# Another order of visits in a weight-gradient kernel that walks PSUM banks by hand

## The chip, the cores and the metric

The kernel runs on one core of a Trainium2 chip. The metric is the device time of one execution in microseconds; the median of three executions of the kernel before is 164.53 us (164.5 to 164.6). The span of the profiled execution, from its first to its last instruction, is 163.0 us.

## The reference

```python
batch, m, k, n = 16, 512, 1024, 768
input:       (batch, m, k) float32
grad_output: (batch, m, n) float32

grad_weight = np.einsum('bmk,bmn->kn', input, grad_output)   # (1024, 768) float32
```

All 16 x 512 = 8192 rows are contracted, so the work is one product of a 1024 x 8192 matrix with an 8192 x 768 matrix.

## The kernel before, in words

**Rows.** The 8192 rows are loaded as 32 loads of 256 rows (u = 0 to 31), input as tile `xp` and gradient as tile `gp`, cast to bf16 on the way by transfers that GpSimd issues (L107 and L108; the first rows come by L82 to L85 and L112 to L114, and rows 0 to 255 of the input are rounded on the chip, L205 to L216 and L361 to L367). `LOADS` says what a load becomes: `s`, two single items of 128 rows each, or `P`, one pair item of 256 rows. Loads 0 to 7 give the single items 0 to 15, loads 8 to 29 the pair items 16 to 37, loads 30 and 31 the single items 38 to 41. Up to 14 loads are held at a time.

**Products.** The output is split into four blocks: A and B are the upper 512 rows, C and D the lower; A and C the left 384 columns, B and D the right. A single item needs a product for each of the four blocks. A pair item is contracted with seven products in place of eight, in the manner of a fast 2 x 2 matrix scheme: `A`, `D`, `m`, `n`, `o`, `p`, `q` (L219 to L240). For that VectorE first makes six sums of a pair item's parts (`sum_g1` to `sum_x3`, L126 to L155, here called a sextet): g1, g2, g3 need the gradient, x1, x2, x3 the input. `o` and `p` need g3; `n` and `q` need x1; `m` needs x1, x2, g1, g2; `A` and `D` need x3 and g1. The five products `m` to `q` are collected in `macc`, and at the end 24 shares (L173 to L190) add them to the blocks in `acc`. Their order is the list `SHARES`.

**Visits.** Each product has 512 x 384 results, which are four PSUM banks (q = 0 to 3) of 128 x 384. Eight banks make two slots of four. A product occupies a slot while its visits run: a visit multiplies some further items of its product, bank by bank, and a closing visit evacuates the banks to `acc` or `macc`. When a product is opened again later, its old sum is either copied into the bank by ScalarE first (L267; the evacuation is then a ScalarE copy, L300), or TensorE starts from zero and VectorE adds the bank to the old sum (L304). Each tile matmul is 128 x 128 by 128 x 384 (L286); there are 936, whatever the order. In the very last visit the last bank is split in two (L333 to L347).

**What sets the order.** Everything is issued in the order of the list `ORDER`, one visit after another, and each engine works through its own queue in that order. A step such as `2A16:3!1,0,3,0` reads: first 2 of VectorE's sums or shares (`fill`, L199); then visit product A up to its item number 16 (in its own list of items: all 42 for A and D, the 20 single ones for B and C, the 22 pairs for `m` to `q`); where this opens the product, 3 of the four banks are done by ScalarE; `!` closes it, with 1, 0, 3 and 0 further sums or shares put ahead of the evacuations of banks 0 to 3. `+n` opens C on top of the finished sum `n`. An item of a visit can only be multiplied when its load has landed and its sums are made; an opened bank must have been evacuated by the visit that held it before. The part that joins VectorE's two kinds of work is

```python
def shut(q):
    fill(ahead[q])
    bank, _, act = banks[q]
    dst = sum_of(p, q)
    if act:
        nc.scalar.copy(out=dst, in_=bank)
    elif fresh[p]:
        nc.vector.tensor_copy(out=dst, in_=bank)
    else:
        nc.vector.tensor_add(out=dst, in0=bank, in1=dst)
```

The list was found by a search over an account of when each transfer lands and how long each operation takes; the kernel holds only its result.

Of the kernel before, what the change touches and what calls it, by code (L numbers as in the profile page):

```python
# [13 lines left out]


ORDER = (
    "C1:4!0,0,0,0 D1:1 A2:2!0,0,0,0 D2!0,0,0,0 B2:2 C3:1 B4!0,0,0,0 C4!0,0,0,0 A3 A4!0,0,0,0 D4 "
    "D5 A6:4!0,0,0,0 D6!0,0,0,0 B6:1!0,0,0,0 C7!0,0,0,0 A8:1 D8:1 D10!0,0,0,0 A10!0,0,0,0 B10:2 "
    "B12!0,0,0,0 C12 D13:3!0,0,0,0 A13:1!0,0,0,0 C16!0,0,0,1 1B16:4!0,0,0,0 D14 2A16:3!1,0,3,0 "
    "D17 3m2:4!2,0,0,1 D18!0,0,0,0 n2:4!1,0,1,0 1q2:4!0,3,0,0 2o3:2 p2:3 o4!0,0,0,1 p4 1A19:4 "  # L20
    "3A20!0,0,3,0 p5 q5!0,0,0,0 m5:4!1,0,2,0 p6!1,1,0,1 n6!0,0,0,1 o6:4 D22:4 9D23 4o8!1,0,0,0 "
    "A24:2!0,0,0,0 2q8:1 q9!1,0,0,0 D25!0,2,0,0 p7 1p8 p10!1,0,2,0 m7:4 m10!0,0,6,0 o11!0,1,0,0 "
    "3n10:4 p12:3!3,1,0,0 n12!1,0,2,0 q12:1 m13:4!6,0,0,0 q13!0,0,0,0 1A28 1A29!0,1,0,2 D30:4 "
    "o14:4 o15!0,1,1,0 D31!0,2,4,0 2p16 1A32:3!0,0,0,0 3n17!0,2,0,1 p17!0,0,0,0 2D33:3 q16:4 "
    "1q18!0,0,1,1 2m16 2D35!0,0,7,0 m19 2m20!0,0,0,0 o20:4 5p19:2 1p21 o21 o22!0,2,0,0 "
    "1p22!0,0,0,3 A36 m22:4!0,0,0,1 A38 q20:3 q22!3,0,0,0 1A40 n20:4 1n22!0,0,0,3 3A42!0,0,1,0 "
    "C20:0+n!0,0,0,1 B20:4!3,1,1,1 D42!0,0,1,0 "
).split()


SHARES = (
    "l20 l21 l22 l23 t10 t11 t12 t13 t20 t21 t22 t30 t31 t32 t23 t33 l30 l10 l11 l12 l31 l32 l13 "
    "l33 "
).split()

# [366 lines left out]
```

## Time and profile before

| | |
|---|---|
| time, median of 3 | 164.53 us |
| span of the profiled execution | 163.0 us |
| TensorE clock granted | 0.999 |
| mean of one tile matmul, start to end (they overlap) | 326 ns |
| addition of a bank to its sum on VectorE (L304) | 549 ns, 96 of them in the largest groups |
| copy of a bank by ScalarE (L300), into a bank (L267) | 490 to 501 ns, 501 to 510 ns |
| sums of a sextet: g1, g2, g3, x1, x2, x3 | 548, 348, 548, 681, 415, 681 ns |
| moved by the DMA engines | 33.40 MB, mean 205 GB/s |

A duration in the profile runs from an instruction's start to its end, and the next one on the same engine may start before that end, so the distances between starts are shorter than the durations. "Idle before" is time in which an engine had nothing to run, with what ended it. For loads the trace also has the time at which the completion of each arrived; "landing" means that time. All times count from the start of the span.

### The profile page before, as it was taken

To read this page: it belongs to the slowest core of one execution; us is meant where nothing else is said; L and a number is where in the kernel's file an instruction comes from. 1 tells how busy PE (TensorE), PEld (TensorE's weight loads), DVE (VectorE), ACT (ScalarE), POOL (GpSimd) and SP (SyncE) were. 2 spreads that over 40 slices of the span, in tenths; PEclk is the share of its full clock that TensorE was granted. 3 is DMA by queue.
4 is the path that set the end of the run, shared out by engine and by line. 5 is a ranking of instruction groups with operands and counts; after the bars stand their busy time and mean duration, and the time that the engine had idled before them with its cause. 6 is when DMAs were issued, how large, how long until landed. Compare 5 with 4: busy or idle time off the path is not lost.

```text
span 163.0 us, 2759 instructions
## 1 busy us (share of the span) xinstructions
PE 158.0 (97%) x955; PEld 93.2 (57%) x955; DVE 130.7 (80%) x271; ACT 96.3 (59%) x226; POOL 34.6 (21%) x69
## 2 busy tenths in 40 slices
PE   8999998999999999999999999999999999999992
PEld 2366664666655656555656555665656566665661
DVE  0458585405969987999799998995998999999992
ACT  3844831347676467955477598549365427877720
POOL 7442222212222222122222222122222000000000
PEclk9999999999999999999999999999999999999999
DMA  5999999999999999999999999999999999600894
GB/s 174 293 212 212 213 212 215 217 211 211 214 215 210 212 211 216 214 211 212 213 214 214 213 211 216 214 211 210 213 216 212 211 213 215 135 4 0 308 322 146
DMA packets 12398, 33.40 MB, mean 205 GB/s; under 512 B 1376, under 2 KB 4192, under 8 KB 12384
## 3 DMA queue, kind: packets, MB, share of 16 engines
q0 software_dynamic: 9360, 28.64, 88.8%
q1 hardware_dynamic: 2592, 3.47, 6.0%
q10 hardware_dynamic: 432, 1.11, 1.8%
q8 instruction: 7, 0.11, 0.3%
q14 instruction: 7, 0.06, 0.1%
HBM read 58.72 MB, written 3.15 MB: 380 GB/s over the span
## 4 chain that ended last, share of the span: by engine, by line
PE 82%; DMA 14%; POOL 1%; issue 1%; DVE 0%; POOLq 0%
PE bank L286 81%; DMA xp<-in_input_dram 14%; POOL gp L112 1%; PE bank L337 0%; DVE acc L345 0%; POOLq L386 0%
## 5 line engine op out<-in xcount | busy, mean ns | idle before, releaser
L286 PEld LDWEIGHTS <-xp 128*128 128x128 bf16 x665 | 64.8, 98 | 45.3 <-DMA xp<-in_input_dram 1.1
L286 PE MATMUL bank<-gp,xp 128*128 128x384 bf16 x492 | 84.0, 326 | 1.1 <-DMA xp<-in_input_dram 0.7
L304 DVE TENSOR_TENSOR acc<-bank,acc 128x384 f32<-128x384 f32 x58 | 29.2, 549 | 16.5 <-PE bank L286 15.9
L300 ACT COPY macc<-bank 128x384 f32<-128x384 f32 x67 | 27.6, 501 | 22.4 <-PE bank L286 22.2
L300 ACT COPY acc<-bank 128x384 f32<-128x384 f32 x54 | 24.0, 490 | 21.2 <-PE bank L286 20.9
L286 PEld LDWEIGHTS <-xe 128*128 128x128 bf16 x264 | 25.7, 98 | 17.5 <-DVE xe L150 0.5
L286 PE MATMUL bank<-ge,xp 128*128 128x384 bf16 x173 | 31.3, 326 | 0.0
L286 PE MATMUL bank<-gp,xe 128*128 128x384 bf16 x176 | 30.5, 326 | 0.0
L108 POOL DMA_DIRECT2D xp<-in_input_dram x30 | 15.9, 530 | 52.3 <-DMA xp<-in_input_dram 28.5
L267 ACT COPY bank<-macc 128x384 f32<-128x384 f32 x50 | 22.6, 510 | 6.2 <-DVE macc L304 4.2
L267 ACT COPY bank<-acc 128x384 f32<-128x384 f32 x45 | 20.4, 501 | 6.7 <-DVE acc L304 3.4
L107 POOL DMA_DIRECT2D gp<-in_grad_output_dram x30 | 15.9, 531 | 38.2 <-DMA gp<-in_grad_output_dram 17.2
L304 DVE TENSOR_TENSOR macc<-bank,macc 128x384 f32<-128x384 f32 x38 | 19.1, 549 | 2.9 <-PE bank L286 1.8
L190 DVE TENSOR_TENSOR acc<-acc,macc 128x768 f32<-128x768 f32 (+1 forms) x24 | 16.5, 748 | 0.0
L286 PE MATMUL bank<-ge,xe 128*128 128x384 bf16 x88 | 15.6, 326 | 0.0
L146 DVE TENSOR_TENSOR xe<-xp 128x1024 bf16<-128x1024 bf16 x22 | 15.0, 681 | 0.7 <-DMA xp<-in_input_dram 0.7
L155 DVE TENSOR_TENSOR xp<-xp 128x1024 bf16<-128x1024 bf16 x22 | 15.0, 681 | 0.0
L132 DVE TENSOR_TENSOR ge<-gp 128x768 bf16<-128x768 bf16 x22 | 12.1, 548 | 0.1
L141 DVE TENSOR_TENSOR gp<-gp 128x768 bf16<-128x768 bf16 x22 | 12.1, 548 | 0.0
L150 DVE TENSOR_TENSOR xe<-xp 128x512 bf16<-128x512 bf16 x22 | 9.1, 415 | 0.0
L136 DVE TENSOR_TENSOR ge<-gp 128x384 bf16<-128x384 bf16 x22 | 7.7, 348 | 0.0
L302 DVE COPY acc<-bank 128x384 f32<-128x384 f32 x7 | 3.5, 550 | 2.5 <-PE bank L286 2.4
(19 smaller groups left out, 21.3 us busy)
## 6 DMA issues: line engine op xcount, KB each, us to landing
xp<-in_input_dram POOLq DMA_DIRECT2D x30, 512.0 KB, 16.8
gp<-in_grad_output_dram POOLq DMA_DIRECT2D x30, 384.0 KB, 16.7
out_dram<-acc SPq DMA_DIRECT2D x15, 192.0 KB, 2.4
xf<-in_input_dram ACTq DMA_DIRECT2D x2, 512.0 KB, 4.9
gp<-in_grad_output_dram POOLq DMA_DIRECT2D x3, 192.0 KB, 6.5
xp<-in_input_dram POOLq DMA_DIRECT2D x2, 256.0 KB, 7.8
gf<-in_grad_output_dram SPq DMA_DIRECT2D x2, 192.0 KB, 4.3
out_dram<-acc SPq DMA_DIRECT2D x1, 128.0 KB, 1.8
```

What stands on the lines that cost most here:

```text
L107: nc.gpsimd.dma_start(out=gp, in_=G[rows, :].rearrange("(p m) n -> p m n", m=2))
L108: nc.gpsimd.dma_start(out=xp, in_=X[rows, :].rearrange("(p m) k -> p m k", m=2))
L132: nc.vector.tensor_add(out=ge[:, 0:2, :], in0=g[:, :, 0, :], in1=g[:, :, 1, :])
L141: nc.vector.tensor_sub(out=g[:, 1:3, :], in0=g[:, 1:3, :], in1=g[:, 3::-3, :])
L146: nc.vector.tensor_add(out=xe[:, 0:2, :].rearrange("p a k -> p (a k)"), in0=xp[:, 0, :], in1=xp[:, 1, :])
L150: nc.vector.tensor_add(out=extra[i][0][:, 2, :], in0=xp[:, 0, 0:KH], in1=xp[:, 1, KH:K])
L155: nc.vector.tensor_sub(out=x[:, 1:3, :], in0=x[:, 1:3, :], in1=x[:, 0::3, :])
L190: op(out=dst, in0=dst, in1=src)
L267: nc.scalar.copy(out=bank, in_=sum_of(p, q))
L286: nc.tensor.matmul(bank, stat, mov, start=opening and j == 0 and not carried, stop=close and j == len(items_now) - 1, skip_group_check=car ...
L300: nc.scalar.copy(out=dst, in_=bank)
L304: nc.vector.tensor_add(out=dst, in0=bank, in1=dst)
```

## The change

`ORDER` and `SHARES` are replaced by other lists; no other line is touched. The new lists come from the same search over an account that differs in two points: it has one transfer landing late, and the third quarter opening later (the words of the change; the diff doesn't say which quarter is meant). The aim is an order that doesn't ask for data before they are there.

Both orders end with the same three products (C, B, D), load the same data in the same sequence and run the same number of tile matmuls. The first difference is in the second visit (`A1` in place of `D1`); around the loads 3 to 5 the single products come in another order; in the middle the products of the pairs are visited in another sequence, with the sums and the shares put at other places among them.

```diff
 ORDER = (
-    "C1:4!0,0,0,0 D1:1 A2:2!0,0,0,0 D2!0,0,0,0 B2:2 C3:1 B4!0,0,0,0 C4!0,0,0,0 A3 A4!0,0,0,0 D4 "
-    "D5 A6:4!0,0,0,0 D6!0,0,0,0 B6:1!0,0,0,0 C7!0,0,0,0 A8:1 D8:1 D10!0,0,0,0 A10!0,0,0,0 B10:2 "
-    "B12!0,0,0,0 C12 D13:3!0,0,0,0 A13:1!0,0,0,0 C16!0,0,0,1 1B16:4!0,0,0,0 D14 2A16:3!1,0,3,0 "
-    "D17 3m2:4!2,0,0,1 D18!0,0,0,0 n2:4!1,0,1,0 1q2:4!0,3,0,0 2o3:2 p2:3 o4!0,0,0,1 p4 1A19:4 "
-    "3A20!0,0,3,0 p5 q5!0,0,0,0 m5:4!1,0,2,0 p6!1,1,0,1 n6!0,0,0,1 o6:4 D22:4 9D23 4o8!1,0,0,0 "
-    "A24:2!0,0,0,0 2q8:1 q9!1,0,0,0 D25!0,2,0,0 p7 1p8 p10!1,0,2,0 m7:4 m10!0,0,6,0 o11!0,1,0,0 "
-    "3n10:4 p12:3!3,1,0,0 n12!1,0,2,0 q12:1 m13:4!6,0,0,0 q13!0,0,0,0 1A28 1A29!0,1,0,2 D30:4 "
-    "o14:4 o15!0,1,1,0 D31!0,2,4,0 2p16 1A32:3!0,0,0,0 3n17!0,2,0,1 p17!0,0,0,0 2D33:3 q16:4 "
-    "1q18!0,0,1,1 2m16 2D35!0,0,7,0 m19 2m20!0,0,0,0 o20:4 5p19:2 1p21 o21 o22!0,2,0,0 "
-    "1p22!0,0,0,3 A36 m22:4!0,0,0,1 A38 q20:3 q22!3,0,0,0 1A40 n20:4 1n22!0,0,0,3 3A42!0,0,1,0 "
-    "C20:0+n!0,0,0,1 B20:4!3,1,1,1 D42!0,0,1,0 "
+    "C1:4!0,0,0,0 A1 D2:3!0,0,0,0 A2!0,0,0,0 B2:1 C3:3 C4!0,0,0,0 B4!0,0,0,0 A3 A4!0,0,0,0 D4 "
+    "B6:3!0,0,0,0 D6 C6:1 C8!0,0,0,0 A8!0,0,0,0 D8 B7:2!0,0,0,0 D10!0,0,0,0 B10:2!0,0,0,0 "
+    "A10!0,0,0,0 B12:2!0,0,0,0 C10 A12 A14!0,0,0,0 D14:2!0,0,0,0 C16!0,2,1,1 B16:4!1,0,1,1 D16 "
+    "A17:4!2,1,1,1 q2:3!0,1,1,1 m2:3!0,0,0,0 D17 p3:3!2,0,1,1 D18!0,0,0,0 n3:4!0,0,0,2 o3:4 "
+    "3A20:3!3,0,0,1 o4 q5:3!2,0,1,2 m5!0,0,0,0 o6!1,1,0,1 n6!1,0,0,0 p6:4 D20:3 D21 5D23 "
+    "3p8!1,1,1,0 A24:2!1,0,1,1 m8:1 2m9!1,0,0,0 D25!0,0,0,1 o9 2o10!2,0,0,0 q9:4 q10!3,1,0,0 "
+    "p11!1,0,0,0 n11:4 5o12:4!3,0,1,0 m12:1 n12!5,0,0,0 m13!0,0,0,0 A27 q13:4!4,0,2,0 A30!1,0,0,1 "
+    "D29:3 p12:4 1p15 D30 6p16!2,1,0,0 D31!0,0,0,1 o16!2,0,1,0 n17:3!0,1,2,2 m16 A32:3!4,0,0,1 "
+    "m18!0,0,0,0 q18 4D35:4!3,0,2,1 q20!0,0,0,0 p19:3 o17:4 3p21 o21 6o22!2,1,0,0 p22!0,0,0,0 A36 "
+    "q22:4!3,1,0,1 1A39 m22:4!1,1,1,1 A40 n22:3!1,2,0,1 A42!2,0,0,0 C20:0+n!0,0,0,1 B20:4!0,1,2,2 "
+    "D42!2,0,0,0 "
 ).split()
...
 SHARES = (
-    "l20 l21 l22 l23 t10 t11 t12 t13 t20 t21 t22 t30 t31 t32 t23 t33 l30 l10 l11 l12 l31 l32 l13 "
+    "l20 l21 l22 l23 t20 t21 t22 t23 t10 t11 t12 t13 t30 t31 t32 t33 l10 l11 l12 l13 l30 l31 l32 "
     "l33 "
 ).split()
```

## The prediction

> **What bounds the kernel now.** I read the engine totals first, then the chain that ended last, the waits, TensorE's timeline around the one long wait, and the busy time by stretches.
>
> ```profile
> PE 158.0 (97%) x955; PEld 93.2 (57%) x955; DVE 130.7 (80%) x271; ACT 96.3 (59%) x226; POOL 34.6 (21%) x69
> ...
> q8 instruction: 7, 0.11, 0.3%
> ```
>
> From the chain (start, duration, what):
>
> ```profile
> 2.41 7.21 DMA xp<-in_input_dram
> 9.62 0.28 issue
> 9.90 15.93 DMA xp<-in_input_dram
> 25.84 0.05 issue
> 25.88 132.81 PE bank L286 x813
> 158.69 0.78 PE bank L337 x7
> ```
>
> The waits (who, for whom: us in total, times, longest; the other engines wait for TensorE, and TensorE's weight loads for one transfer) and TensorE's timeline:
>
> ```profile
> DVE acc L304 <- PE bank L286: 15.9, 10, 3.7
> ...
> PEld L286 <- DMA xp<-in_input_dram: 1.1, 1, 1.1
> ```
>
> ```profile
> 16.69 8.45 PE L286 MATMUL bank<-gp,xp 128*128 128x384 bf16 x51
> 25.88 4.40 PE L286 MATMUL bank<-gp,xp 128*128 128x384 bf16 x26 [0.74 <-DMA xp<-in_input_dram]
> ```
>
> Until 25.88 us the end is set by a load (pair u=4: items 8 and 9); after it TensorE runs 813 matmuls without a long stop. The records start 162 or 163 ns apart when nothing waits. I use 0.1624 us and call p the number of tile matmuls ahead of one. The first (p=0) starts at 5.44 us, so 5.44 + 0.1624p is the time without any wait, and the **lag** is what a matmul starts later than that. From the records: lag 0.70 at p=88, 1.60 at p=116 (25.88 us), 1.84 at p=364, 1.94 at p=540, 2.14 at p=740, 2.22 at p=908. So before loses 0.70 at the start, 0.90 to the late load, and 0.62 afterwards: 0.53 in nine waits of 0.02 to 0.13 us, the rest because 0.1624 is a little short. These 2.22 us are all that an order of visits can win: there are 936 tile matmuls, 152.0 us, in any order.
>
> VectorE is the next engine to look at (busy time by stretches; columns PE, PEld, DVE, ACT, POOL):
>
> ```profile
> 100.00:110.00 10.00, 10.00 (x63) 6.03 (x62) 9.86 (x22) 5.54 (x14) 2.37 (x5) 1.00 1.07 213
> ...
> 140.00:150.00 10.00, 10.00 (x63) 6.01 (x62) 9.79 (x15) 7.24 (x19) 0.00 (x0) 1.00 0.13 27
> ```
>
> It is nearly full there, though TensorE hardly waits for it.
>
> **What the Trainium skill says.** "TensorE: Matmul & The Clock Gate", Back-to-back issue gap, prices one matmul of N columns at N/2.4 + 2.5 ns: 162.5 ns for 384, and the trace has 162 to 163. "Perfetto Trace Analysis", Identifying the Most-Contended Engine, warns that matmul busy time doesn't tell how near the limit TensorE is; hence start distances here, not the 97%. "DMA: Bandwidth & Descriptors", Why a DMA increments its semaphore by 16, says that 16 engines finish a transfer independently and only all 16 make it landed; its Queues, rings and completion order says that an engine takes turns between queues, packet by packet. The trace fits both: a 16 KB packet of the instruction queue starts at 21.27 us and takes 945 ns, and the gradient load of u=4 lands at 23.48, 2.98 us after the one before it where 1.85 is usual. The loads behind it keep their 4.31 us a pair but stay that much late. Which DMA engine it was the records don't say, so the cause is a reading. The diff doesn't touch what I take for the trigger (the length of TensorE's program), so I keep the landings of before: u=3 at 20.49, u=4 at 25.84, then 4.31 us a pair; u=29 (item 37) at 133.70, u=31 at 142.33.
>
> **The change part by part.** Nothing is removed but waits: 936 matmuls, the 22 sextets of sums and the 24 shares stay. Counted from the two strings: openings 57 to 58; preloads by ScalarE 99 both; evacuations by ScalarE 121 to 120; by VectorE 107 to 112 (97 to 101 additions, 10 to 11 copies). VectorE starts such evacuations 0.465 us apart, so it gets 5 x 0.465 = 2.3 us more work. Walking each engine's queue with TensorE's positions as the clock:
>
> *Start.* A1 instead of D1 takes the left half of the gradient, which is rounded earlier, so the 0.30 us wait for the right half (6.57 us) goes. But D2 then meets item 1's gradient, landed at 7.46: its second matmul (p=9) starts at 7.51 where before had 7.58. Gain 0.07.
>
> *The late transfer.* C8 (p=88) comes at 7.51 + 79 x 0.1624 = 20.34, 20.37 with a 0.03 wait of C3 for a bank, and needs u=3: 20.54 with 0.05 from landing to matmul. Lag 0.81: a wait of 0.17 that before doesn't have (C7 reaches that load two matmuls later). Behind it on TensorE stand A8, D8 and B7, and the evacuations of C8 on VectorE wait with them; none of these has work that something else is short of then. D10, the first to need u=4, moves from p=116 to p=124, behind A8, D8 and B7, which use u=3 and older: 20.54 + 36 x 0.1624 = 26.39 us, after the landing. The 0.74 us of idle time is gone. At p=124 the lag is 0.81 against 1.62.
>
> *The middle.* With lag 0.81 loads are met with less in hand. VectorE's sextet starts as the load lands, and I compare its ends with the first matmul that needs them (starts 0.469, 0.269, 0.469, 0.602, 0.336, 0.602 apart). A24: x of item 23 lands at 73.30, its three sums end 73.35 + 0.60 + 0.34 + 0.68 = 74.97, 75.01 with the semaphore; p=423 comes at 74.95: 0.06 to 0.10 late. p11: the four additions of o10 and four sums put item 26 (p=498) 0.09 late. m13 0.12, A30 0.17, n17 0.16 are late against a lag of 0.81, but these too wait for landings, and vanish once the lag has grown by 0.2. Everything else has room. The same walk of the order of before gives 0.05, 0.10, 0.06, 0.07, 0.05 and 0.06 where its trace has small waits, so I add 0.10 for what it misses: lag at the end 0.81 + 0.10 + 0.09 + 0.05 (matmuls are nearer 162.45) + 0.10 = 1.15.
>
> *Item 37.* o22 (p=784, both orders) can't run before 133.75, which is a lag of 0.99 whatever comes earlier. So the lag at the end lies between 1.0 and 2.22, unless the new order has large waits of its own.
>
> *The end.* From the landing of x37 VectorE has 3 sums (1.54), 12 wide shares (0.869), 12 narrow ones (0.469) and 15 evacuations: 1.54 + 10.43 + 5.63 + 6.98 = 24.6 us, to 158.3. TensorE ends near 158.6, so the last addition still waits for it, and the tail (additions, stores, 3.4 us after the last matmul's start) is the same. The buffers of pairs and sums are freed over 15 us before they are needed in both orders, so no load starts later.
>
> Sum: 164.53 - (2.22 - 1.15) = 163.46, say **163.5 us**.
>
> **The rivals.** *The waits come back (chance 0.12).* Visits that open a slot with none in between go from 6 to 8, with A17, q2, m2 three in a row, and the sextets are laid out with 0.1 us to spare. For it: the nine small waits of before. If they double to 1.2 us, the lag ends at 0.81 + 1.2 = 2.0: 164.3, still less than before but near no change. *The late transfer moves or comes twice (0.09).* If instruction fetches hit one DMA engine again, landings are 1 us later, o22 is held to lag 2.0 and the time is 164.3 to 164.5. Against it: no such shift in the six later 16 KB packets. *VectorE becomes the bound (0.06), slower.* Its 2.3 us of new work all lengthen the path: 163.5 + 2.3 = 165.8. For it: 9.8 of 10 us busy in two stretches. Against it: its sums wait for landings in my walk, 1.2 us ahead of x37 alone. *All small waits hide (0.03):* lag 1.0, 163.3.
>
> **How the numbers follow.** My forecast has 0.70. Range 163.1 to 164.3: from 0.2 under the o22 bound (landings moved by that much) to the half-lost gain. Below 164.2 counts as faster: 0.70, 0.03 and most of the first rival, 0.84; the same 0.10; slower 0.06.
>
> **What would show it.** No TensorE wait for a load near 25 us; one of about 0.2 near 20.5; a lag of 0.8 at p=124; u=4 still at 25.8; item 37 met by TensorE with no time in hand at 133.8; VectorE busy near 133. Wrong would be a second late transfer, a wait over 0.2 us for VectorE between 40 and 130 us, or VectorE running past TensorE at the end.

## The result

The changed kernel takes 164.06 us (median of 6 executions, 163.87 to 164.22), the kernel before 164.55: a ratio of 0.9968, 95% interval 0.9955 to 0.9981. In a second comparison, on another occasion, it was 163.95 against 164.67, 0.9955 (0.9941 to 0.9968). So it is faster by 0.5 to 0.7 us, where 1.05 had been forecast. The direction and most of the mechanism were right, and the time lies in the range; the gain is about half to two thirds of the forecast. One execution in the experiments below (of the kernel with the old opening and the new rest) took 429.87 us; no figure here includes it, and its cause is not known.

### The profile page after: what moved, and what is told of

Read it like the earlier page. It is cut to its first block, busy times and chain, and to the rows that moved or that the text cites. A ratio compares the mean times of both kernels' runs of the same rounds, so it can differ in the third digit from the quotient of the medians.

```text
span 162.3 us, 2773 instructions
## 1 busy us (share of the span) xinstructions
PE 158.0 (97%) x955; PEld 93.6 (58%) x955; DVE 134.1 (83%) x276; ACT 96.4 (59%) x225; POOL 34.7 (21%) x69
## 4 chain that ended last, share of the span: by engine, by line
PE 92%; DMA 4%; DVE 1%; issue 1%; ACT 0%; ACTq 0%; POOLq 0%
PE bank L286 92%; DMA gp<-in_grad_output_dram 4%; PE bank L337 0%; DVE acc L345 0%; DVE acc L304 0%; ACT bank L267 0%; ACTq L267 0%; POOLq L386 0%
## 5 line engine op out<-in xcount | busy, mean ns | idle before, releaser
L286 PE MATMUL bank<-gp,xp 128*128 128x384 bf16 x492 | 85.2, 327 | 0.4 <-ACT bank L267 0.2
L300 ACT COPY macc<-bank 128x384 f32<-128x384 f32 x67 | 29.1, 494 | 27.6 <-PE bank L286 27.2
L304 DVE TENSOR_TENSOR acc<-bank,acc 128x384 f32<-128x384 f32 x62 | 31.5, 550 | 12.7 <-PE bank L286 12.2
L286 PEld LDWEIGHTS <-xe 128*128 128x128 bf16 x264 | 25.8, 98 | 17.1
L300 ACT COPY acc<-bank 128x384 f32<-128x384 f32 x53 | 23.5, 486 | 19.0 <-PE bank L286 18.7
L286 PE MATMUL bank<-ge,xp 128*128 128x384 bf16 x173 | 32.1, 326 | 0.0
L267 ACT COPY bank<-macc 128x384 f32<-128x384 f32 x50 | 21.9, 515 | 0.1
L90 PE MATMUL bank<-const-bfloat16-1.0 128*128 128x512 bf16 (+1 forms) x12 | 4.6, 577 | 0.8 <-PEq L386 0.8
```

What stands on the lines that cost most here:

```text
L267: nc.scalar.copy(out=bank, in_=sum_of(p, q))
L286: nc.tensor.matmul(bank, stat, mov, start=opening and j == 0 and not carried, stop=close and j == len(items_now) - 1, skip_group_check=car ...
```

## The profile after

Engine totals and the instruction queue, from the page of the changed kernel:

```profile
PE 158.0 (97%) x955; PEld 93.6 (58%) x955; DVE 134.1 (83%) x276; ACT 96.4 (59%) x225; POOL 34.7 (21%) x69
...
q8 instruction: 7, 0.11, 0.3%
```

TensorE has the same instructions and the same busy time. VectorE has 5 instructions and 3.4 us more (134.1 for 130.7), ScalarE one copy less. The counts are those of the prediction; its 2.3 us for VectorE were reckoned from the distances between starts. The chain that ended last (start, duration, what):

```profile
1.23 6.45 DMA gp<-in_grad_output_dram
7.67 0.04 issue
7.72 13.03 PE bank L286 x79
20.75 0.01 issue
20.75 15.79 PE bank L286 x96
36.54 0.55 DVE acc L304
37.09 0.02 issue
37.11 0.02 ACTq L267
37.12 0.35 issue
37.47 0.49 ACT bank L267
37.97 0.04 issue
38.01 120.05 PE bank L286 x737
```

Before, loads stood in the chain until 25.88 us. Now it leaves them at 7.67 us, where item 1's gradient lands; after that TensorE gives way only twice in this chain, at 20.75 us (the load 3 that C8 meets) and at 38.01 us. The second is new: VectorE adds a bank of A14, ScalarE copies D14's old sum into the freed bank, and 0.35 us of that is "issue", time for which the profile shows no reason. TensorE's timeline shows no wait where it had stood idle for 0.74 us, near 25 us:

```profile
16.68 13.51 PE L286 MATMUL bank<-gp,xp 128*128 128x384 bf16 x81
```

and two of its waits (who, for whom: us in total, times, longest):

```profile
PEld L286 <- DMA xp<-in_input_dram: 0.6, 2, 0.4
PE bank L286 <- ACT bank L267: 0.2, 1, 0.2
```

The second is the wait at 38.01 us (p=192, in D14). The view counts from the end of the matmul ahead, which overlaps the next one. From start to start the distance is 0.346 us longer than the usual 0.1624, and this is what the text below calls a wait.

VectorE in the two stretches that were shown of before (columns PE, PEld, DVE, ACT, POOL):

```profile
100.00:110.00 10.00, 10.00 (x64) 6.01 (x62) 8.96 (x20) 5.34 (x13) 2.61 (x5) 1.00 1.07 213
140.00:150.00 10.00, 10.00 (x64) 6.04 (x62) 10.00 (x16) 8.14 (x20) 0.00 (x0) 1.00 0.14 28
```

In the second of them VectorE is busy all the time, and TensorE never waits for it there.

Lags, as the prediction defined them (start of the matmul less 5.44 + 0.1624p), from the records:

| | before | forecast | changed, first trace | changed, second trace |
|---|---|---|---|---|
| p=9 (item 1's gradient has landed) | 0.68 | 0.61 | 0.82 | 0.61 |
| p=88 (C7 or C8) | 0.70 | 0.81 | 1.02 | 0.81 |
| p=124 (behind the late load) | 1.62 | 0.81 | 1.03 | 0.83 |
| p=200 (behind D14) | 1.62 | 0.81 | 1.39 | 1.18 |
| p=784 (item 37) | 2.16 | 0.99 or more | 1.57 | 1.37 |
| p=908 (last visit) | 2.22 | 1.15 | 1.58 | 1.38 |

The executions in these traces took 164.76 us (before), 164.11 and 163.95. In all ten traces of this study the time of the execution is 162.53 to 162.67 us plus its lag at p=908, so the lag accounts for nearly all of the differences. Before's trace is not a typical one: its execution is 0.2 us above the median.

The second trace follows the forecast to 0.02 us until p=124, then loses 0.35 between there and p=200, where nothing had been expected, and 0.20 in the remaining 708 matmuls, where before lost 0.60. The first trace has the same and 0.21 more from its start, because item 1's gradient landed at 7.67 us and not at 7.47.

## The experiments

**The changed kernel again.** No edit. Is the wait at D14 the program's?

> The changed kernel once more, nothing altered. Theory 1 (the wait at D14 belongs to the program: ScalarE refills banks 2 and 3 of D14 only when VectorE has added A14's last banks): TensorE again waits about 0.35 us near 38.0 us, and the time is 164.0 to 164.2. Rival (an accident of that one execution): the wait there is under 0.05 us and the profiled time nearer 163.7. In both: the second wait at the start is ended by the landing of item 1's gradient, which came at 7.67 us in the changed kernel's trace and at 7.46 in that of before; if the difference is chance it will fall anywhere between.

Measured 163.95 us, 0.9955 (0.9941 to 0.9968), the second comparison above. The wait at p=192 is 0.346 us in both traces. ScalarE's timeline in this one (idle time and what ended it in brackets):

```profile
37.27 0.89 ACT L267 COPY bank<-acc 128x384 f32<-128x384 f32 x2 [4.22 <-DVE acc L304]
```

The refill starts 0.37 us after the record of its wait (36.90 us), again. So the wait is the program's. The landing of item 1's gradient is not: 7.47 us here, and between 7.38 and 7.96 in the ten traces of this study, which issue it at the same time.

**D14 without ScalarE.**

```diff
- ... A14!0,0,0,0 D14:2!0,0,0,0 C16!0,2,1,1 ...
+ ... A14!0,0,0,0 D14!0,0,0,0 C16!0,2,1,1 ...
```

> The changed kernel with D14 opened without ScalarE: its four banks start from zero and VectorE adds them, 2 more additions (0.93 us) and 4 fewer copies on ScalarE. Theory 1 (the refill's chain costs 0.35 us and nothing takes it back): the wait at 38.0 us is gone and the time falls by 0.3 to 163.7 or 163.8. Rival (what TensorE wins there it loses again to loads and sums before item 37, or VectorE's two additions delay the sums that C16 carries): 164.0 to 164.2, with new waits between 40 and 134 us.

Measured 163.57 us, 0.9939 (0.9927 to 0.9952), less than the changed kernel in the same comparison by 0.38 us (medians) or 0.26 (ratios). TensorE runs through. The longest piece of its chain is

```profile
8.00 150.01 PE bank L286 x920
```

where the changed kernel's chain had pieces of 79, 96 and 737 matmuls. Between p=200 and 908 it loses 0.20 us, as the changed kernel does. The profiled execution itself took 164.09; in it item 1's gradient landed at 7.96 us, 0.5 later than in the changed kernel's second trace, which is about the whole difference. TensorE therefore reaches p=200 no earlier than in that trace (lag 1.33 against 1.18); that an earlier arrival is kept as well, the next run shows. This run takes the refill away altogether, so it doesn't tell whether the chain or the 0.35 us of "issue" was at fault.

**Why ScalarE is late.** In the changed kernel's two traces, and in those of two orders below that keep D14's refill, the late instruction is number 63 of ScalarE's records, counted from 0 with its waits and DMA issues. Number 319 in the changed kernel (near 154.3 us) and number 191 in three of the orders below start as late after the record of their wait: steps of 128. The edit puts two instructions ahead:

```diff
+    spare = accp.tile([P, 8], f32, name="spare")
...
+        if n == 10:
+            for c in range(2):
+                nc.scalar.copy(out=spare[:, c : c + 1], in_=nc.const_aps.tensor(1.0, (P, 1), bf16))
```

> The changed kernel with two copies of one column into a tile that nothing reads, on ScalarE ahead of D4 (near 14.6 us, where ScalarE is idle). In three traces the refill of D14's bank 2 starts 0.37 us after the semaphore it waits for, where other refills take 0.03 to 0.09, and it is ScalarE's instruction 63 counted from 0 each time; instruction 319 = 63 + 256, and in one order 191 = 63 + 128, show the same. Theory (ScalarE changes to its next 128 instructions there, whatever they do): with two more instructions ahead the delay goes to the copy before (near 32.5 us, which nobody waits for), the wait at D14 falls from 0.35 to under 0.06, and the time by 0.3, to 163.65. Rival (the delay belongs to this refill, say to 4 us of idle time before it or to its bank): wait and time as in the changed kernel, 163.95.

Measured 163.62 us, 0.9943 (0.9930 to 0.9955). ScalarE's timeline, in the changed kernel's first trace and in this one (where all lines of the file are one or more further down):

```profile
32.39 0.86 ACT L300 COPY acc<-bank 128x384 f32<-128x384 f32 x2 [1.00 <-PE bank L286]
37.47 0.90 ACT L267 COPY bank<-acc 128x384 f32<-128x384 f32 x2 [4.22 <-DVE acc L304]
```

```profile
32.20 0.48 ACT L301 COPY acc<-bank 128x384 f32<-128x384 f32 x1 [1.00 <-PE bank L287]
32.84 0.48 ACT L301 COPY acc<-bank 128x384 f32<-128x384 f32 x1 [0.17 <-ACT acc L301]
36.97 0.94 ACT L268 COPY bank<-acc 128x384 f32<-128x384 f32 x2 [3.64 <-DVE acc L305]
```

The copy before, which ran on without a gap in the changed kernel, now starts 0.17 us after the end of the one ahead, and it is number 63. The refill now starts 0.06 us after the record of its wait (36.91 us), although ScalarE was again idle for over 3 us before it, so neither the idle time nor the bank is the reason. TensorE's wait at p=192 falls from 0.346 to 0.036, and its chain is again one piece of 920 matmuls. Its lag is 0.88 at p=200 and 1.07 at p=908: again 0.20 lost, so the lead is kept. More work on ScalarE made the kernel 0.2 (by the ratios) to 0.3 us (by the medians) faster.

The ten traces together say when the delay shows. Nine times a copy with one of these numbers stands directly behind a record that waits for a semaphore, on an idle ScalarE; all nine start 0.32 to 0.37 us after the end of that record. With other numbers there are 358 such copies, and all start within 0.05 us. (Twice more, in orders below, number 191 stands behind such a record while the copy ahead still runs.) Where the number falls into a run of copies without gaps (63 in the kernel before), no delay is seen, nor where the copy itself waits without a record ahead (191 in this run starts 0.02 us after its semaphore).

**The old opening with the new rest.**

```diff
- the new order up to D14
+ the old order up to B12 C12 D13:3!0,0,0,0 A13:1!0,0,0,0
  C16!0,2,1,1 B16:4!1,0,1,1 D16 A17:4!2,1,1,1 q2:3!0,1,1,1 ...
```

> The kernel before up to D13 and A13, and from C16 on the new order (D16 and A17 take one more item each to bridge). If the lags add up: the middle of the new order has 0.20 us of waits where the old has 0.60, so 0.4 less than before, 164.15; TensorE still waits 0.74 us for load 4 near 25.1 us. Rival (the middle is only free of waits because the new opening gives it other sums in hand): 164.5, no change.

Measured 164.18 us, 0.9968 (0.9958 to 0.9979). The stop for load 4 is there:

```profile
25.68 1.64 PE L285 MATMUL bank<-gp,xp 128*128 128x384 bf16 x9 [0.53 <-DMA xp<-in_input_dram]
```

and after p=124 only 0.21 us are lost, to a lag of 1.63. The calm middle belongs to the new order of the pair products, whichever opening is ahead of it. It alone is worth 0.4 us by the lags (0.60 - 0.21) and 0.5 by the times. In this trace load 4's input landed at 25.64 us (25.84 in that of before), so the stop itself was 0.2 shorter.

**The new opening with the old rest.**

```diff
  the new order up to A14!0,0,0,0 D14:2!0,0,0,0
+ C16!0,0,0,1 1B16:4!0,0,0,0 D15 2A16:3!1,0,3,0
+ D17 3m2:4!2,0,0,1 ... as before
```

> The kernel before with the new order up to A14 and D14 (and D15 in place of D14 as the bridge), all after that as before. If the traces' lags add up: the opening won 0.64 by D10 and lost 0.35 at D14, so 0.3 less than before, 164.25. Rival (the middle of the old order has more waits when it comes earlier, since loads are met with less in hand): 164.4 or more.

Measured 165.66 us, 1.0060 (1.0047 to 1.0072): slower than before. The lead at p=240 is 0.43 us (lag 1.23 against 1.66), and 1.13 are lost at p=246 to 261: 0.37 in A16, whose banks are refilled while only D15's four matmuls run, and 0.76 in m2, for which x1 and x2 of item 17 come late (VectorE makes them from 49.10 us; before, from 48.36). Two items that now stand ahead had pushed A16's evacuation back, and the sums behind it in VectorE's queue with it. That is the bridge's fault, so a second attempt took the sums from the new order:

```diff
- C16!0,0,0,1 1B16:4!0,0,0,0 D15 2A16:3!1,0,3,0
+ C16!0,2,1,1 B16:4!1,0,1,1 D15 A16:3!1,0,0,0
```

> The new opening with the old rest once more, but with the seven sums put where the new order has them (in C16 and B16) and not where the old one had them (in A16). If the 1.1 us of waits of the first attempt (p=246 to 261) came from sums that stood behind the later evacuation of A16, they shrink to 0.3 or less and the time is 164.3 to 164.5; if the old middle can't follow the new opening at all, they stay and it is over 165.

Measured 164.80 us, 1.0010 (1.0004 to 1.0017). The 0.76 is gone, the 0.37 at A16 stayed, and neither range was met. The rest went at p=549, where the old order loses 0.02 and this one 0.18:

```profile
46.76 49.83 PE bank L286 x303
96.59 0.02 issue
96.61 62.14 PE bank L286 x380
```

The wait at 96.61 is for a bank that ScalarE refills at the end of a run of copies; in that run, at 94.16 us, stands ScalarE's number 191, directly behind the record of a wait. It starts 0.55 us after the copy ahead of it, where this run of copies otherwise has 0.37 and less, so 0.18 late. The first attempt has the same late copy and the same wait. That this is the cause is argued from the traces and wasn't tried. So the opening alone brings nothing here: its lead of half a microsecond is used up at the junction and at p=549. What it is worth in front of the rest that was searched for it is the difference between the old and the new opening there: 164.18 - 163.95 = 0.23 us, and 0.4 (by the ratios) to 0.6 us (by the medians) without the wait at D14.

**The late transfer.**

```diff
-WARMUP = [512] * 10 + [128] * 2
+WARMUP = [128] * 42
```

> The kernel before with its warm-up as 42 matmuls of 128 columns in place of 10 of 512 and 2 of 128: the same columns, 30 more pairs of weight load and matmul, so all of TensorE's later instructions are 60 further on. Theory (the late landing of load 4 comes from the 16 KB fetch of TensorE's instructions at 21.27 us): the fetch comes 30 matmuls earlier, near 16.4 us, and it is the gradient or input of load 3 that lands about 1 us late, with load 4 the usual 1.85 behind it. Rival (load 4 is late of itself, by its place in the ring of GpSimd's transfers): the step of 2.7 to 3.0 us stays ahead of load 4's gradient. In both the stop near 25.8 us stays, and the time too, within 0.5 us.

The first 16 KB packet of the instruction queue starts at 15.59 us (21.27 before). Now it is load 2's input that lands late, at 17.63 us, 3.91 after its gradient where 2.45 is usual; load 4's gradient comes the usual 1.86 after load 3. TensorE's timeline:

```profile
13.72 3.09 PE L286 MATMUL bank<-gp,xp 128*128 128x384 bf16 x18
17.67 2.61 PE L286 MATMUL bank<-gp,xp 128*128 128x384 bf16 x15 [0.86 <-DMA xp<-in_input_dram]
```

So which load is late goes by TensorE's count of instructions, as the reading in the prediction had it, and not by the load. The stop of 0.9 us moved with it, to D5; that it would stay near 25.8 us was wrong. The kernel takes 165.22 us, 1.0044 (1.0026 to 1.0062), 0.6 more than before where at most 0.5 had been expected. Its lag at p=124 is 1.86 against 1.62, as the step is larger here; its other three executions were slower than the one in the trace, and why isn't shown. That the packet holds up one DMA engine remains a reading; no record names the engine.

**An attempt at a better order.**

```diff
- ... D6 C6:1 C8!0,0,0,0 A8!0,0,0,0 D8 B7:2!0,0,0,0 ... D14:2!0,0,0,0 ...
+ ... D6 A6!0,0,0,0 C8:1!0,0,0,0 A8!0,0,0,0 D8 B7!0,0,0,0 ... D14!0,0,0,0 ...
```

> An attempt at a better order: D14 without ScalarE as before, and ahead of load 3 A6 (items 4 and 5) is visited, so that C8 meets load 3 two matmuls later; B7 without ScalarE. Theory (TensorE's lag is the sum of its waits until item 37 sets a floor): the wait of 0.16 us near 20.5 goes, and 163.4 is reached against 163.55 for D14 alone. Rival (the floor of item 37, or the 6 more additions on VectorE near 22 us): 163.55 or more, with a wait at p=784 or near B7.

Measured 163.68 us, 0.9943 (0.9929 to 0.9956): no better than D14 alone. The time is the rival's, but not by the waits it named: there is none at p=784 or at B7. The wait at p=88 is gone, but TensorE loses 0.36 us after p=124 in place of 0.21 to 0.24, the largest part (0.13 at p=322) for a sum of item 19. TensorE is hardly earlier there than in the run with two spare copies (lag 0.85 at p=200, against 0.88). It is the loads that are later in this execution: item 1's gradient landed at 7.64 us and load 4's input at 25.87, against 7.47 and 25.51. VectorE starts item 18's sums as its input lands, goes on without a gap, and ends item 19's at 58.66 in place of 58.33. So with so little lag, a late landing comes back as a wait for sums. Whether this order is better when the loads land early isn't shown.

## Why the prediction was right, and where its size was off

*The bound.* Right. TensorE's work is the same and only waits were to be won; the lags tell the time of every profiled execution to 0.14 us. One remark on the 162.5 ns: the section of the Trainium skill they come from ("TensorE: Matmul & The Clock Gate", Back-to-back issue gap) gives its formula for an isolated matmul and says that it counts too much for a stream of weight loads and matmuls with many columns. This kernel is such a stream, with 384 columns, and its starts are 162 to 163 ns apart, so here the formula holds.

*The start.* Right, but for chance. A1 needs nothing that is late, and TensorE stops at p=9 for item 1's gradient, 7.51 us in the second trace, as worked out. The prediction took its landing as fixed at 7.46; it was 7.67 in the first trace, and all of the 0.21 stayed to the end.

*The late transfer.* Right in each part: C8 waits 0.16 to 0.17 (0.17 forecast), load 4 lands late as before (25.79 and 25.65 us), D10 doesn't wait for it, and p=124 comes at 26.41 us in the second trace where 26.39 was forecast. Of the cause that the prediction read into it, the fetch of TensorE's instructions, the run with the longer warm-up list confirms the place: it goes by TensorE's count. That the fetch itself holds the load back stays a reading.

*The step that failed* is "Everything else has room". It stands for D14, where the walk of the queues saw no wait worth naming. It was 0.346 to 0.360 us, in all four traces that have this refill as ScalarE's number 63. The chain was right (A14's addition, then the refill, then the matmul), with next to no time in hand; the price of the refill's start was wrong. I took it to start as its semaphore comes; it starts 0.37 us later there, since it is number 63 of ScalarE's records and stands behind the record of a wait. With that delay moved to a copy that nobody waits for, the lag at the end is 1.07 (1.15 forecast) and the time 163.62, a gain of 0.9 to 1.0 us (0.9943) against the forecast 1.05.

*The start of the sum* was off too. The prediction took 2.22 - 1.15 from 164.53, a median, but the lag of 2.22 is that of an execution of 164.76 us. A lag of 1.15 goes with 163.69 (164.76 - 1.07), not with 163.46. From there the second comparison closes: 0.35 for D14's refill, less 0.09 for small waits that were allowed for and didn't come, gives the 163.95 that was measured. So of the 0.49 us between 163.46 and 163.95, 0.23 comes from mixing two executions, and the rest is the refill. The first comparison's trace has 0.2 more from the landing of one transfer.

*The middle.* Right in kind, a little too dear: 0.29 was allowed for waits after p=200, 0.20 was lost. p11 has 0.05. A24 has 0.05 too, but not the wait that was foretold for it: it comes five matmuls later, for a bank that ScalarE refills, and before has the same one. m13, A30 and n17 don't wait, as expected once the lag is larger.

*The rivals.* Waits did come back, as the first has it, but one large one, not a doubling of the small ones; the small ones fell from nine with 0.53 us to three with 0.13. The late transfer neither moved nor came twice. VectorE did get its additional work, is full between 140 and 150 us, and is not the bound: TensorE doesn't wait for it there. Not all small waits hid. Item 37's floor (lag 0.99) was approached by the run with two spare copies, 1.06, and not reached; the changed kernel comes to item 37 with a lag of 1.37, so the sign that TensorE meets it with no time in hand did not show.

## What to carry to other kernels

When the busiest engine is nearly full, write down how late it is against its own rate, step by step, and take the time from the same execution as the lags: the few places where that lag grows are all there is to win, and the same list tells afterwards which term was mis-sized. A chain through three engines that ends just in time is not free: price the start of each operation in it, too, and look in a trace for the longest start and not the usual one. And an order that was searched as a whole is not made of parts: half of it in front of the other half can be slower than the old one, because sums and evacuations share a queue.

## What the runs showed of the hardware that was not expected

- ScalarE can start late at every 128th of its records. Numbers 63, 191 and 319 start 0.32 to 0.37 us after the end of the semaphore wait's record directly ahead of them (nine of nine on an idle ScalarE), where 358 copies with other numbers take 0.04. Two instructions more ahead move the delay by two. No delay is seen where the number falls on a copy that runs on without a gap, or that waits without such a record. What ScalarE does then isn't shown by any record; that it goes by its own count is.
- A 16 KB packet of the instruction queue comes about once in 250 records of TensorE, and with the first of them a load lands about 1 us late (2.68 to 3.03 us between load 3 and load 4's gradient in nine traces, against 1.86 in the one where the packet comes earlier). The later loads keep their pace and stay late. After the six later packets a single landing is late by up to 0.8 us (3.26 us behind the one ahead for 2.45, with two spare copies), but the next makes most of it up: from load 4's input to the last load the ten traces differ by no more than 0.35 us.
- Item 1's gradient, for which TensorE waits at p=9, landed between 7.38 and 7.96 us in kernels that issue it at the same time. In this kernel such a difference goes straight to the end, and it is as large as the change's own gain.
